# A decoder layer's delta rule on one core: triangular inverse merged to 128 rows, key norms from the Gram diagonal, local logits ahead of the inverse

## Chip, cores and metric

One Trainium2 chip, one of its cores. The metric is the device time of one execution in microseconds; it was 1342.42 us (median of three runs, 1338.79 to 1344.01).

## What is computed

One decoder layer in float32, 256 tokens of width 2048. The mixer has eight heads of a gated delta rule and eight heads of causal local attention; then come an output projection, cross-attention to 256 memory tokens, a gated MLP with a causal convolution, and norms. The change lies in the two kinds of mixer heads:

```
q, k, v = silu(conv(.)) per head;  k and q scaled to length 1
A = strictly lower part of (beta k) k^T * decay      (chunks of 64 tokens)
T = inverse of (I + A)
v_new = T (beta v) - T (beta k exp(G)) state
o = q exp(G) state + (q k^T * decay) v_new
state = state * exp(G_last) + (k exp(G_last - G))^T v_new
local head:  softmax(q k^T / sqrt(128) + bias) v, causal
```

The kernel uses two token blocks of 128 in place of four chunks of 64; the result is the same.

## The kernel before

All weights come once from HBM, 1 MB a transfer, into three raw buffers. A weight tile (a unit: 8 k-tiles of 128 columns, or 2 of 512) is split into a high part `hi` (ScalarE, ACT) and a rest `lo` (VectorE, DVE), each in a ring of four tiles. TensorE (PE) multiplies hi by the whole of the other side and lo by its high part: per k-tile one product of 512 columns and one of 256. These form the weight stream; `stream` (L275) writes it in order.

Everything else is written as jobs: Python generators (`k_evac`, `q_evac`, `v_evac`, `kb_evac`, `mem_job` and others) that yield wherever a result must come back from another engine. `Plan` (L48) keeps a rough clock of the engines while the program is written; `Jobs.tick` lets a job go on when its last result is due by that clock, so its instructions land between the products of the stream. All engines then run their instructions in the order in which they were written. The clock counts for a transfer 0.25 us and its size, and then 2.2 us until its data is there (`Plan.dma`).

The parts that matter here:

- Keys (`k_evac`, L572). After convolution and SiLU the squares of k (ACT) are summed over the channels by two products with a column of ones on PE; then come the Gram products k k^T of both token blocks, in the same bank.
- Inverse (`subst_job`, `u_job`, L616 and L653). DVE substitutes blocks of 32 rows; `u_job` joins two blocks of 32 to one of 64, with two pairs of products on PE. So `U` holds inverses of 64 rows.
- Values (`v_evac`, L727). For each of two token blocks a head applies the inverse: first 64 rows, a product with the off-diagonal block of 64, a subtraction, a product with the second inverse of 64, so three products with a copy or a subtraction after each; then the output and its norm (`out_norm`).
- Local attention (`kb_evac`, L821). A head waits until all inverses are there (`done["U"]`), makes logits, takes a tile of 128x512 from the pool `T5` (four tiles, tt0 to tt3) for bias, exponent and transposes, and multiplies by the values; heads 4 to 7 wait before that for all heads' `y`.
- Memory tokens (`mem_job`, `mem_piece`, L944 and L957). When heads of the delta rule are done, their tiles are reused for the transposed memory tokens, 16 k-tiles in tiles mT0 (0 to 5), mT1 (6 to 11) and mT2 (12 to 15). A piece is two k-tiles: it takes a T5 tile if another one is free too (`T5.get(1)`), SyncE (SP) transfers 256 KB into it, and ACT and DVE split it into mT. The four memory blocks of the stream (`mk_evac`), first k-tiles 0 to 7 of all four, then 8 to 15, follow the mixer's input projection. `when` holds the writing of a product back until its source has been written; on the chip PE then waits for it.

SP's queue holds both kinds of transfers: a weight load goes out when its raw buffer has been split, and the loads and pieces behind it wait for that.

Of the kernel before, what the change touches and what calls it, by code (L numbers as in the profile page):

```python
# [33 lines left out]
# columns of the small per-channel tensor  # L34
# [3 lines left out]
# columns of the constant tensor  # L38
# [9 lines left out]
class Plan:  # L48
    """A rough clock of the engines, kept while the program is written: a job goes on when its last
    result is due, so that no engine waits in its queue for another."""  # L50
# [17 lines left out]
    def dma(self, queue, size):  # L68
        """A transfer; returns when its data is there."""
        c, start = self.cur, max(self.t.get(queue, 0.0), self.now)  # L70
        if c is not None and c.eng != queue:
            start = max(start, c.end + SEM)
        self.t[queue] = start + 0.25 + size / 380e3
        if c is not None:
            c.end, c.eng = self.t[queue] + 2.2, queue
        return self.t[queue] + 2.2
# [107 lines left out]
def layer_kernel(ctx: ExitStack, tc: tile.TileContext, ins, out):  # L184
# [18 lines left out]
    # ---------------- tiles that live through the kernel  # L203
# [34 lines left out]
    # ---------------- the weight stream  # L238
# [56 lines left out]
    def w_unit(src, steps):  # L295
        """128-column blocks of weights as the stationary side, tokens moving; steps: (block, k)."""
        def tick(i):
            def f(u):
                for j in range(i, min(i + 2, len(steps))):
                    b, k = steps[j]  # L300
                    if k == 0:
                        b["ps"] = now(acc)
                    ps, last = b["ps"], k == b["k"] - 1
                    w = slice(j * P, (j + 1) * P)
                    xk = src(k)
                    if b["wide"]:
                        mm(ps, u.hi[:, w], xk, start=k == 0, stop=False)
                    else:
                        mm(ps[:, :256], u.hi[:, w], xk[:, :256], start=k == 0, stop=False)
                        mm(ps[:, :256], u.hi[:, w], xk[:, 256:], start=False, stop=False)  # L310
                    mm(ps[:, :256], u.lo[:, w], xk[:, :256], start=False, stop=last)
                    if last:
                        jobs.add(b["evac"](ps))
            return f
        return Unit(len(steps) * P, [tick(i) for i in range(0, len(steps), 2)])
# [20 lines left out]
    def s_block(src, kts, cols, evac, size=2, first=0):  # L336
        """Some k-tiles of weights per unit moving, the tokens stationary."""
        box = {}
        g = [kts[i:i + 1] for i in range(first)] + [kts[i:i + size] for i in range(first, len(kts), size)]
        return [Unit(len(ks) * cols, [s_part(src, ks, k, cols, box, ks is g[0], ks is g[-1]) for k in ks],  # L340
                     after=(lambda: evac(box["ps"])) if ks is g[-1] else None) for ks in g]

    def s_block_last(src, kts, cols, evac):
        """As s_block; the last units serve the first token block, and then the second."""
# [22 lines left out]
    # ---------------- small helpers  # L367
    def rstd_of(ss, n, w, tag=None):
        """(ss / n + eps) ** -0.5 for [P, w]."""
        r = stat(w, tag)  # L370
        vec.tensor_scalar(r, ss, 1.0 / n, EPS, op0=OP.mult, op1=OP.add)
        pool.tensor_tensor(r, r, pw[:, :w], op=OP.pow)
        return r

    def split(dst, ps, g=None):
        """PSUM [P, 256] -> high and low parts of dst [P, 512]."""
# [11 lines left out]
    # ---------------- start: constants, x, its norm and transposes  # L388
# [28 lines left out]
    # gst columns: 0:2 |k|^2 + eps, 2:4 beta / that, 6:8 its root, 10:12 |q|^2 + eps, 12:14 scale of q,  # L417
    # 14:16 sum of o^2, 16:20 the output's factor
    done = {"y": 0, "L": 0, "Q": 0, "U": 0, "T": False, "bt": False, "oT": 0, "oTm": 0, "d": 0, "mk": 0}

    # ---- w_in stream
    def when(key, ap):
        """The source of a product, once the program that writes it is there."""
# [123 lines left out]
    def conv_front(ps, blk, taps, dst_fn):  # L547
        """Evacuate a channel-major block, convolve over tokens, SiLU."""
# [23 lines left out]
    def k_evac(h):  # L572
        def f(ps):
# [11 lines left out]
            act.activation(t1[:, :256], kT, AF.Square)  # L585
            yield
# [3 lines left out]
            for tb in range(2):  # L590
                mm(ps[:, 384 + tb:385 + tb], t1[:, tb * P:(tb + 1) * P], ones[:, :1])
            mm(ps[:, :256], kT[:, :P], kT)
            mm(ps[:, 256:384], kT[:, P:], kT[:, P:])
            yield
            T.put(t1)
            vec.tensor_scalar(st[:, 0:2], ps[:, 384:386], EPS, None, op0=OP.add)
# [56 lines left out]
    def u_job(h):  # L653
# [16 lines left out]
        vec.tensor_tensor(u, u, ps[:, 256:].rearrange("p (b c) -> p b c", b=2), op=OP.subtract)  # L670
        aux.put(ps)
# [31 lines left out]
    def out_norm(ps, st, c_in, f_of, sink, g, z=None):  # L703
        """PSUM [tok, 2, 128] of one head -> RMS norm (and gate) -> channel-major high and low parts."""
        t = yield from T.get()
# [21 lines left out]
    def v_evac(h):  # L727
        def f(ps):
# [18 lines left out]
            for tb in range(2):  # L747
                c = slice(tb * P, (tb + 1) * P)
                lc = tb * 256
# [9 lines left out]
                act.activation(y[:64, c], ps[:64, :P], AF.Copy)  # L759
                yield  # L760
                mm(ps[64:, P:256], l[:64, lc + 64:lc + P], y[:64, c])
                yield
                vec.tensor_tensor(v[64:, c], v[64:, c], ps[64:, P:256], op=OP.subtract)
                yield
                mm(ps[64:, 256:384], u[64:, 64:], v[64:, c])
                yield
                act.activation(y[64:, c], ps[64:, 256:384], AF.Copy)
                yield
                aux.put(ps)
            T.put(v)  # L770
# [23 lines left out]
            yield from out_norm(ps, st, 14, f_of, sink, gcol(G_GDN, 0), [d[:, 384:], l[:, 384:512]])  # L794
# [26 lines left out]
    def kb_evac(h):  # L821
        def f(ps):
# [3 lines left out]
            while ("qb", h) not in box or not done["bt"] or done["U"] < H:  # L826
                yield
# [24 lines left out]
            while h >= H // 2 and done["y"] < H:  # L852
                yield
            ps = yield from aux.get()
# [23 lines left out]
            yield from out_norm(ps, st, 4, f_of, sink, gcol(G_MOBA, 0))  # L878
# [4 lines left out]
    # ---------------- residual blocks  # L883
    def resid_evac(n, ver, gbase, wide):
        """x += product, channel-major; high and low parts with the next norm's gain."""
# [13 lines left out]
    def x_rstd(ver):  # L899
        """The factors [P, 2] of the norm of x, from its channel-major blocks."""  # L900
# [24 lines left out]
    # ---------------- memory tokens  # L925
    def natural_ss(src, tile, ss):
        """Sums of squares of the rows [tokens, D], one 512-column piece in tile after another."""
# [121 lines left out]
    # ---------------- gated MLP  # L1049
# [61 lines left out]
    def final(tb, ps):  # L1111
        """The last columns of a token block, the final norm and the store."""
# [22 lines left out]
    # ================= the stream of weights, in the order of use  # L1135
# [76 lines left out]
    # ================= emission  # L1212
# [10 lines left out]
    def row_tile(r):  # L1223
        """The per-token factors r [P, 2] along the free axis, on every partition."""
# [120 lines left out]
# ---- host side: layouts only  # L1345
def _w(w):
    """[2048, 128 n] -> n blocks [2 halves, 128, 8 * 128]: the units of w_block."""
# [4 lines left out]
def _s(w):  # L1352
    """[k, 512 n] -> n blocks [k / 256, 128, 2 * 512]: the units of s_block."""
# [4 lines left out]
def _t(x):  # L1358
    """[tokens, D] -> [128, D / 128, tokens]."""
# [97 lines left out]
```

## Time and profile before

| | us |
|---|---|
| three runs | 1338.79, 1342.42, 1344.01 |
| profiled execution, span from first to last instruction | 1340.8 |
| PE busy in it | 1325.9 (99%) |
| DVE busy | 933.6 (70%) |
| ACT busy | 687.9 (51%) |
| GpSimd (POOL) busy | 53.0 (4%) |

The profiled execution has no time of its own beside its span. It is one execution, and busy time of PE is the union of its instructions, whose ends are modelled. In the timeline the distance from one start to the next is the better measure of what an instruction costs. All instructions are recorded under line 95, the line of the helper that issues them, so groups are told apart by tiles: bank is a PSUM bank, t and tt are scratch tiles, U and kt the inverses and their transposes, AB the heads' decay and Gram matrices, ytiles the values' y.

### The profile page before, as it was taken

Reading aid. Unit: us, or ns where it says so; the run is one execution under the profiler, and the core shown is the slowest. Engines: PE = TensorE matmul, PEld = TensorE weight load, DVE = VectorE, ACT = ScalarE, POOL = GpSimd, SP = SyncE. Lnnn points to the kernel's source line nnn. Section 1 sums busy time; section 2 is a strip of 40 time slices with the busy share of each in tenths; the row PEclk is TensorE's granted clock in tenths of the full one; section 3 lists DMA queues with packets and bytes.
Section 4 is the critical chain, followed back from the end, with each engine's and each line's share of the span. In section 5 each row is a group of like instructions: output and inputs, shape, how many; then the busy total and the mean of one; then the engine's idle time right before and its main releaser. Section 6 shows DMA issues by size and latency. Waiting matters only on the chain.

```text
span 1340.8 us, 19353 instructions
## 1 busy us (share of the span) xinstructions
PE 1325.9 (99%) x7414; PEld 1150.0 (86%) x7414; DVE 933.6 (70%) x1594; ACT 687.9 (51%) x1112; POOL 53.0 (4%) x140
## 2 busy tenths in 40 slices
PE   8999999999999999999999999999999999999997
PEld 7998888888888889998888888888888888888886
DVE  5688798968786766687777777545477777775554
ACT  5676554557564544465544444433344444444443
POOL 0101110201110000000000000000000000000000
PEclk9999999999999999999999999999999999999999
DMA  9666555534255654455455555555545555555552
GB/s 328 220 225 212 191 210 188 183 117 150 95 197 187 224 196 179 157 194 184 160 187 187 188 183 196 188 189 188 188 173 188 195 199 185 192 189 189 188 188 95
DMA packets 50793, 250.43 MB, mean 187 GB/s; under 512 B 11603, under 2 KB 15884, under 8 KB 23436
## 3 DMA queue, kind: packets, MB, share of 16 engines
q1 hardware_dynamic: 49152, 245.53, 51.5%
q0 software_dynamic: 448, 2.11, 0.4%
q10 hardware_dynamic: 1100, 1.54, 0.4%
q8 instruction: 58, 0.95, 0.3%
q14 instruction: 35, 0.29, 0.1%
HBM read 246.53 MB, written 2.64 MB: 186 GB/s over the span
## 4 chain that ended last, share of the span: by engine, by line
PE 54%; issue 0%; DVE 0%; ACT 0%; POOLq 0%; POOL 0%; ACTq 0%; DVEq 0%
PE bank L95 54%; ACT xn L95 0%; DVE lo L95 0%; ACT hi L95 0%; DVE xn L95 0%; DVE t L95 0%; POOLq L1453 0%; POOL stats L95 0%; DVE tt L95 0%; ACTq L95 0%; DVE stats L95 0%; DVEq L95 0%
## 5 line engine op out<-in xcount | busy, mean ns | idle before, releaser
L95 DVE TENSOR_TENSOR lo<-raw,hi 128x1024 fp32r<-128x1024 f32 (+4 forms) x449 | 540.2, 1205 | 349.1 <-ACT hi L95 344.8
L95 PE MATMUL bank<-xT,hi 128*128 128x512 f32 x2112 | 754.7, 400 | 0.3 <-DVE xT L95 0.3
L95 ACT ACTIVATE hi<-raw 128x1024 fp32r<-128x1024 f32 (+4 forms) x449 | 467.2, 1042 | 468.0 <-PE bank L95 357.7
L95 PE MATMUL bank<-xT,lo 128*128 128x256 f32 x2112 | 592.3, 280 | 0.0
L95 PEld LDWEIGHTS bank<-xT,hi 128*128 128x128 f32 x2112 | 396.3, 188 | 92.6 <-issue 2.6
L95 PEld LDWEIGHTS bank<-xT,lo 128*128 128x128 f32 x2112 | 399.3, 189 | 0.6
L95 PE MATMUL bank<-hi,actT 128*128 128x512 f32 x704 | 221.0, 395 | 0.0
L95 PEld LDWEIGHTS bank<-hi,actT 128*128 128x128 f32 x704 | 132.3, 188 | 31.5
L95 PE MATMUL bank<-lo,actT 128*128 128x512 f32 x352 | 139.0, 395 | 0.0
L95 PE MATMUL bank<-hi,xT 128*128 128x512 f32 (+3 forms) x320 | 87.2, 357 | 4.0 <-ACT xT L95 3.2
L95 DVE SCALAR_TENSOR_TENSOR t<-pad,sml,t 128x256 f32<-128x256 f32 x160 | 78.6, 491 | 8.5 <-DVE t L95 0.9
L95 PEld LDWEIGHTS bank<-lo,actT 128*128 128x128 f32 x352 | 66.2, 188 | 15.8
L95 ACT ACTIVATE t<-bank 128x256 f32<-128x256 f32 (+1 forms) x164 | 56.6, 348 | 21.4 <-PE bank L95 21.2
L95 PEld LDWEIGHTS bank<-hi,xT 128*128 128x128 f32 x320 | 57.4, 192 | 10.1 <-ACT xT L95 3.9
L95 ACT ACTIVATE t<-t,sml 128x256 f32<-128x256 f32 x44 | 22.3, 506 | 78.5 <-DVE t L95 78.4
L95 DVE TENSOR_TENSOR t<-bank,t 128x256 f32<-128x256 f32 x132 | 55.1, 417 | 3.4 <-ACT t L95 3.3
L95 PE MATMUL bank<-lo,xT 128*128 128x512 f32 (+3 forms) x160 | 56.3, 352 | 0.0
L95 POOL TENSOR_TENSOR stats<-stats,pw 128x2 f32<-128x2 f32 (+1 forms) x38 | 29.4, 775 | 557.5 <-DVE stats L95 557.5
L95 PE MATMUL bank<-oTm,hi 128*128 128x512 f32 x128 | 45.1, 394 | 0.0
L95 PE MATMUL bank<-oTg,hi 128*128 128x512 f32 x128 | 45.1, 393 | 0.0
L95 DVE TENSOR_TENSOR t<-t,t 128x256 f32<-128x256 f32 x96 | 41.0, 427 | 1.8
L95 PE MATMUL bank<-oTg,lo 128*128 128x256 f32 x128 | 36.2, 283 | 0.0
(157 smaller groups left out, 1053.8 us busy)
## 6 DMA issues: line engine op xcount, KB each, us to landing
raw<-wst SPq DMA_DIRECT2D x212, 1024.0 KB, 4.8
raw<-wz SPq DMA_DIRECT2D x4, 768.0 KB, 4.4
raw<-wz SPq DMA_DIRECT2D x3, 800.0 KB, 8.6
xn<-x SPq DMA_DIRECT2D x4, 512.0 KB, 8.4
raw<-wz SPq DMA_DIRECT2D x4, 512.0 KB, 4.4
tt<-mem SPq DMA_DIRECT2D x8, 256.0 KB, 5.1
tt<-memT SPq DMA_DIRECT2D x8, 256.0 KB, 5.9
xres<-xT SPq DMA_DIRECT2D x4, 512.0 KB, 5.8
```

The lines of the kernel that those rows point to most:

```text
L95: r = f(o, *a, **k)
```

## The change

1. `k_evac`: the squares on ACT and the two one-column products per head are gone. The norm is read off the Gram matrix: two DVE instructions multiply a 128x128 block of the bank by the identity and sum each row.
2. `u_job` goes on from 64 to 128 rows: two transposes of 64x64, a copy, two products of 64x64 with 64 columns, a copy, two more such products, a subtraction, for each head. `v_evac` then applies the inverse with one product per token block, and the two products of 64x64 with 128 columns, their copy and subtraction are gone.
3. `kb_evac` makes logits, exponent and transposes without the inverse, and waits for `done["U"]` after them; its tile for the norm is taken ahead of the bank. `out_norm` gets its tile from the caller, v in a head of the delta rule.

```diff
@@ k_evac
             t1, kT = yield from conv_front(ps, h, 4, lambda: box["kt"][:, h, :])
-            act.activation(t1[:, :256], kT, AF.Square)
-            yield
             while ("d", h) not in box:
                 yield
             ps = yield from aux.get()
-            for tb in range(2):
-                mm(ps[:, 384 + tb:385 + tb], t1[:, tb * P:(tb + 1) * P], ones[:, :1])
             mm(ps[:, :256], kT[:, :P], kT)
             mm(ps[:, 256:384], kT[:, P:], kT[:, P:])
             yield
+            for tb in range(2):
+                stt(t1[:, tb * P:(tb + 1) * P], ps[:, tb * 256:tb * 256 + P], 1.0, ident, OP.mult, OP.mult,
+                    accum_out=st[:, tb:tb + 1])
             T.put(t1)
-            vec.tensor_scalar(st[:, 0:2], ps[:, 384:386], EPS, None, op0=OP.add)
+            vec.tensor_scalar(st[:, 0:2], st[:, 0:2], EPS, None, op0=OP.add)
@@ u_job
         vec.tensor_tensor(u, u, ps[:, 256:].rearrange("p (b c) -> p b c", b=2), op=OP.subtract)
+        yield
+        for tb in range(2):
+            pe.transpose(ps[:64, tb * 64:tb * 64 + 64], U[:64, tb * H + h, :64], ident[:64, :64])
+        yield
+        act.activation(t[:64, :P], ps[:64, :P], AF.Copy)
+        yield
+        for tb in range(2):
+            mm(ps[64:, P + tb * 64:P + tb * 64 + 64], l[:64, tb * 256 + 64:tb * 256 + P], t[:64, tb * 64:tb * 64 + 64])
+        yield
+        act.activation(t[64:, :P], ps[64:, P:256], AF.Copy)
+        yield
+        for tb in range(2):
+            mm(ps[:64, 256 + tb * 64:256 + tb * 64 + 64], t[64:, tb * 64:tb * 64 + 64], U[64:, tb * H + h, 64:])
+        yield
+        w = U[:64, h:2 * H:H, 64:]
+        vec.tensor_tensor(w, w, ps[:64, 256:384].rearrange("p (b c) -> p b c", b=2), op=OP.subtract)
@@ v_evac
                 mm(ps[:, :P], u, v[:, c])
                 yield
-                act.activation(y[:64, c], ps[:64, :P], AF.Copy)
-                yield
-                mm(ps[64:, P:256], l[:64, lc + 64:lc + P], y[:64, c])
-                yield
-                vec.tensor_tensor(v[64:, c], v[64:, c], ps[64:, P:256], op=OP.subtract)
-                yield
-                mm(ps[64:, 256:384], u[64:, 64:], v[64:, c])
-                yield
-                act.activation(y[64:, c], ps[64:, 256:384], AF.Copy)
+                act.activation(y[:, c], ps[:, :P], AF.Copy)
                 yield
                 aux.put(ps)
-            T.put(v)
...
-            yield from out_norm(ps, st, 14, f_of, sink, gcol(G_GDN, 0), [d[:, 384:], l[:, 384:512]])
+            yield from out_norm(v, ps, st, 14, f_of, sink, gcol(G_GDN, 0), [d[:, 384:], l[:, 384:512]])
@@ kb_evac
-            while ("qb", h) not in box or not done["bt"] or done["U"] < H:
+            while ("qb", h) not in box or not done["bt"]:
                 yield
...
-            while h >= H // 2 and done["y"] < H:
-                yield
+            while done["U"] < H or (h >= H // 2 and done["y"] < H):
+                yield
+            t = yield from T.get()
             ps = yield from aux.get()
```

Since the jobs are written by the clock of `Plan`, the change moves many other instructions. Three places follow, as the programs have them; raw0 to raw2 are weight buffers, tt0 to tt3 the T5 tiles, memT the transposed memory tokens in HBM, mT0 to mT2 their split tiles; the number behind the underscore tells allocations of a name apart.

SP's queue at the end of the mixer's input projection, before:

```order
L95 DMA raw1_73<-wst 128x2048
L95 DMA tt2_104<-memT 128x512
L95 DMA tt3_105<-memT 128x512
L95 DMA raw2_74<-wst 128x2048
L95 DMA raw0_72<-wst 128x2048
L95 DMA tt1_103<-memT 128x512
L95 DMA tt2_104<-memT 128x512
L95 DMA tt3_105<-memT 128x512
L95 DMA raw1_73<-wst 128x2048
```

and now:

```order
L95 DMA raw0_72<-wst 128x2048
L95 DMA raw1_73<-wst 128x2048
L95 DMA tt0_102<-memT 128x512
L95 DMA tt1_103<-memT 128x512
L95 DMA raw2_74<-wst 128x2048
L95 DMA tt2_104<-memT 128x512
L95 DMA raw0_72<-wst 128x2048
L95 DMA tt1_103<-memT 128x512
L95 DMA raw1_73<-wst 128x2048
L95 DMA tt2_104<-memT 128x512
```

Both listings hold the last five of memT (mT1 and mT2). Before, two weight loads stood between the second and the third, and the last three followed each other; now a load stands ahead of each of the last three, and the last piece (tt2, k-tiles 14 and 15) stands behind a load of raw1.

PE in the first memory block, around k-tiles 6 and 7 (the first rows with mT1), before:

```order
L95 MATMUL bank5_111<-mT0_2846,lo1_80 128x256
L95 MATMUL bank5_111<-mT0_2846,hi1_76 128x512
L95 MATMUL bank5_111<-mT0_2846,lo1_80 128x256
L95 MATMUL bank0_106<-cst_68,tt0_102 128x128 x3
L95 MATMUL bank5_111<-mT1_3253,hi1_76 128x512
L95 MATMUL bank5_111<-mT1_3253,lo1_80 128x256
L95 MATMUL bank5_111<-mT1_3253,hi1_76 128x512
L95 MATMUL bank5_111<-mT1_3253,lo1_80 128x256
L95 MATMUL bank6_112<-cst_68,t10_94 128x128 x2
```

and now:

```order
L95 MATMUL bank5_111<-mT0_3071,hi1_76 128x512
L95 MATMUL bank5_111<-mT0_3071,lo1_80 128x256
L95 MATMUL bank5_111<-mT0_3071,hi1_76 128x512
L95 MATMUL bank5_111<-mT0_3071,lo1_80 128x256
L95 MATMUL bank5_111<-mT1_3327,hi1_76 128x512
L95 MATMUL bank5_111<-mT1_3327,lo1_80 128x256
L95 MATMUL bank6_112<-t6_90,t10_94 128x128
L95 MATMUL bank6_112<-t6_90,t10_94 128x256
L95 MATMUL bank5_111<-mT1_3327,hi1_76 128x512
L95 MATMUL bank5_111<-mT1_3327,lo1_80 128x256
```

Before, the two k-tiles follow each other; now a group of logits (t6, t10) stands between k-tile 6 and k-tile 7.

DVE around the splits of mT2 (k-tiles 12 to 15), before:

```order
L95 SCALAR_TENSOR_TENSOR mT2_3353<-tt2_104,sml_69,mT2_3353 128x256
L95 TENSOR_TENSOR lo3_82<-raw2_74,hi3_78 128x1024
L95 SCALAR_TENSOR_TENSOR mT2_3353<-tt3_105,sml_69,mT2_3353 128x256
L95 TENSOR_SCALAR t10_94<-bank6_112,stats_101 128x128 x2
L95 SCALAR_TENSOR_TENSOR mT1_3253<-tt1_103,sml_69,mT1_3253 128x256
L95 TENSOR_TENSOR lo0_79<-raw2_74,hi0_75 128x1024
L95 TENSOR_TENSOR t11_95<-bank1_107,t11_95 128x256
L95 SCALAR_TENSOR_TENSOR mT2_3353<-tt2_104,sml_69,mT2_3353 128x256
L95 SCALAR_TENSOR_TENSOR mT2_3353<-tt3_105,sml_69,mT2_3353 128x256
```

and now:

```order
L95 TENSOR_TENSOR lo3_82<-raw1_73,hi3_78 128x1024
L95 COPY tt0_102<-bank6_112 128x384
L95 TENSOR_TENSOR lo0_79<-raw1_73,hi0_75 128x1024
L95 RECIPROCAL stats_101<-stats_101 128x2
L95 TENSOR_TENSOR stats_101<-stats_101 128x2
L95 SCALAR_TENSOR_TENSOR stats_101<-stats_101 128x2
L95 TENSOR_SCALAR stats_101<-stats_101 128x2
L95 SCALAR_TENSOR_TENSOR mT2_3422<-tt1_103,sml_69,mT2_3422 128x256 x2
L95 TENSOR_SCALAR t8_92<-bank7_113,stats_101 128x128 x2
L95 SCALAR_TENSOR_TENSOR oTm1_3526<-bank7_113,sml_69,oTm1_3526 128x256
L95 SCALAR_TENSOR_TENSOR mT2_3422<-tt2_104,sml_69,mT2_3422 128x256 x2
```

Before, mT2 is written around the splits lo3 and lo0 of the units that PE starts on after 1792 and 1808 products of the stream; now it is written after lo3 and lo0 of the units at 1856 and 1872. PE wants k-tile 12 at product 1832 and k-tile 14 at 1836 in both.

## Rows read from the trace of the kernel before

**Rows 1.** The page, part 1: busy us (share of the span) xinstructions.

```profile
PE 1325.9 (99%) x7414; PEld 1150.0 (86%) x7414; DVE 933.6 (70%) x1594; ACT 687.9 (51%) x1112; POOL 53.0 (4%) x140
```

**Rows 2.** Windows, mid-program: stretch and length, PE, PEld, DVE, ACT, POOL, clock, DMA.

```profile
450.00:475.00 25.00, 25.00 (x144) 21.93 (x143) 16.77 (x23) 12.36 (x15) 0.00 (x0) 1.00 0.56 201
```

**Rows 3.** Waits of PE: waiter, releaser: total us, times, longest us.

```profile
PE bank L95 <- ACT xT L95: 3.2, 1, 3.2
```

**Rows 4.** Windows at the start, columns as in rows 2.

```profile
8.00:12.90 4.90, 0.99 (x5) 0.40 (x3) 2.38 (x4) 3.05 (x5) 0.00 (x0) 1.00 1.03 401
13.40:16.70 3.30, 3.30 (x12) 3.26 (x11) 3.26 (x6) 2.56 (x6) 0.00 (x0) 0.50 1.02 394
```

**Rows 5.** Timeline of PE: start us, us, instruction; Gram group and logits group.

```profile
109.55 0.50 PE L95 MATMUL bank<-ones,t 128*128 128x1 f32 x4
...
110.88 0.28 PE L95 MATMUL bank<-xT,lo 128*128 128x256 f32 x1
...
356.88 0.82 PE L95 MATMUL bank<-t,t 128*128 128x128 f32 x4
...
357.76 0.28 PE L95 MATMUL bank<-xT,lo 128*128 128x256 f32 x1
```

**Rows 6.** Timelines of DVE and PE: a split lo and its first use.

```profile
104.34 1.22 DVE L95 TENSOR_TENSOR lo<-raw,hi 128x1024 fp32r<-128x1024 f32 x1
...
106.72 0.40 PE L95 MATMUL bank<-xT,hi 128*128 128x512 f32 x1
```

**Rows 7.** Timeline of PE: runs of 64x64 in the stream.

```profile
320.30 0.28 PE L95 MATMUL bank<-xT,lo 128*128 128x256 f32 x1
320.51 0.43 PE L95 MATMUL bank<-ytiles,AB 64*64 64x128 f32 x2
...
321.21 0.28 PE L95 MATMUL bank<-xT,lo 128*128 128x256 f32 x1
...
287.23 1.08 PE L95 MATMUL bank<-ytiles,AB 64*64 64x128 f32 x8
...
288.58 0.28 PE L95 MATMUL bank<-xT,lo 128*128 128x256 f32 x1
```

**Rows 8.** Groups by form, whole program: xcount, busy us, mean ns, idle before.

```profile
L95 PE MATMUL bank<-t,U 64*64 64x128 f32 x32 | 5.8, 287 | 0.0
L95 PEld LDWEIGHTS bank<-ytiles,AB 64*64 64x64 f32 x32 | 3.2, 132 | 1.9 <-issue 0.7 <-ACT hi L95 0.3 <-ACT t L95 0.3
L95 PEld LDWEIGHTS bank<-ones,t 128*128 128x128 f32 x64 | 8.8, 190 | 0.9
L95 DVE SCALAR_TENSOR_TENSOR t<-bank,stats,AB 128x128 f32<-128x128 f32 x16 | 4.6, 344 | 0.8 <-POOL stats L95 0.8
L95 ACT ACTIVATE hi<-raw 128x1024 fp32r<-128x1024 f32 x424 | 448.6, 1059 | 455.3 <-PE bank L95 350.9 <-issue 88.8 <-ACT t L95 4.4
L95 ACT ACTIVATE mT<-tt,sml 128x256 fp32r<-128x256 f32 x16 | 7.5, 503 | 1.2 <-DMA tt<-memT 1.0
L95 DVE TENSOR_TENSOR lo<-raw,hi 128x1024 fp32r<-128x1024 f32 x424 | 519.5, 1226 | 334.1 <-ACT hi L95 329.8 <-PE bank L95 3.1
```

**Rows 9.** Timelines of DVE and PE: last split of mT, first use.

```profile
396.35 0.87 DVE L95 SCALAR_TENSOR_TENSOR mT<-tt,sml,mT 128x256 fp32r<-128x256 f32 x2
...
409.91 0.48 PE L95 MATMUL bank<-mT,hi 128*128 128x512 f32 x1
```

**Rows 10.** DMA issues: count, KB each, median us to landing.

```profile
raw<-wz SPq DMA_DIRECT2D x4, 768.0 KB, 4.4
raw<-wz SPq DMA_DIRECT2D x3, 800.0 KB, 8.6
tt<-memT SPq DMA_DIRECT2D x8, 256.0 KB, 5.9
```

**Rows 11.** Timelines of SP and ACT: three pieces of memT and the first's split.

```profile
382.92 1.58 SPq L95 DMA_DIRECT2D tt<-memT  x3
...
388.61 1.16 ACT L95 ACTIVATE mT<-tt,sml 128x256 fp32r<-128x256 f32 x2 [0.19 <-DMA tt<-memT]
```

More of the change, by code (lines that the diff above doesn't have):

```diff
@@ L701, in q_evac, with out_norm @@
         return f
-    def out_norm(ps, st, c_in, f_of, sink, g, z=None):
-        t = yield from T.get()
+    def out_norm(t, ps, st, c_in, f_of, sink, g, z=None):
         for tb in range(2):
@@ L748, in f @@
                 c = slice(tb * P, (tb + 1) * P)
-                lc = tb * 256
                 u = U[:, tb * H + h, :]
@@ L876, in sink @@
                 return box[n][:, h % 4, :]
-            yield from out_norm(ps, st, 4, f_of, sink, gcol(G_MOBA, 0))
+            yield from out_norm(t, ps, st, 4, f_of, sink, gcol(G_MOBA, 0))
             done["oTm"] += 1
```

## The prediction

> **What bounds the kernel now.** I read the page first. TensorE (PE) is busy for 1325.9 of 1340.8 us [rows 1], and the clock is full in its middle part [rows 2]. "Busy" can hide waits, since matmul ends are modelled, so I went to the waits of PE next: the longest single one is 3.2 us [rows 3], and it lies at the start, where PE has little to do [rows 4]. Then the timeline of PE, where I took times from start to start: in a plain stretch 144 products of the weight stream pass in 25 us [rows 2], 0.174 us each, and the small products of the attention are slipped in between with no gap that a wait would leave. So in the part that the change touches PE is the bound: an instruction taken from PE is worth its own length, and a wait put before one costs its whole length. What VectorE (DVE) and ScalarE (ACT) gain or lose is worth nothing while their splits of the weights stay ahead of PE.
>
> **The change, part by part.**
>
> *Norm of k.* Eight heads lose four one-column instructions each (two products, each issued as two). With them the inserted group lasts from 109.55 to 110.88 us, 1.33 us; a group that holds only the four logit instructions, of the same shapes as the four Gram instructions, lasts from 356.88 to 357.76, 0.88 us [rows 5]. That is 0.45 us a head, **3.6 us off PE**. ACT loses eight squares. DVE gets 16 products with the identity, priced like the nearest form that reads PSUM, 0.344 us [rows 8]: 5.5 us in all, 0.69 a head. I cost them at nothing. What hides them is DVE's lead: the thinnest that I found is the split that ends at 104.34 + 1.22 = 105.6 and is first used at 106.72 [rows 6], 1.2 us, and the new order puts two blocks of decay products, which stood ahead of that split, behind it. Without that lead the added 0.69 us a head would stall PE, 5.5 us in all.
>
> *The inverse.* Products of 64x64 are dear because of the change of shape. Two such instructions put 0.21 + 0.70 - 0.35 = 0.56 us into the stream, where 0.35 is what the two neighbours take without them (2 x 0.174); eight last from 287.23 to 288.58, 1.35 us against 0.70 for two, so one more costs 0.108 us and one run 0.56 - 2 x 0.108 = 0.34 us on top [rows 7]. Before there are 64 such instructions (two groups of 32, of which one stands in [rows 8]) in 20 runs, counted on the timeline: 64 x 0.108 + 20 x 0.34 = 13.7 us. The change removes all and adds 64 of 64 columns and 16 small transposes; in the new order they stand in 15 runs. The price of 64 columns is not in the trace. At most it is that of 128, 0.108; at least half, 0.054. I take the half, because the weight load of a 64x64 instruction is also shorter, 132 against 190 ns [rows 8], so it would not bind. So 80 x 0.054 + 15 x 0.34 = 9.4 us, **4.3 us off PE**; with the upper price 13.7, nothing gained. Three ACT and three DVE steps per half and head leave the chain of the values; PE never waited for them, so I give nothing for it.
>
> The Trainium skill, page "TensorEngine Tiling (Array Packing)", section "Restrictions and Gotchas", says that column tiling switches off the transpose mode for FP32. By it the 16 transposes would be issued as ordinary products, 16 instructions more, and the sum would be 16 x 0.054 = 0.9 us higher by my estimate. No row here shows a 64x64 transpose, and the sum goes without it.
>
> *Logits earlier.* They cost PE the same. But a head of local attention now takes its T5 tile, and keeps it, before it waits for the inverse. There are four such tiles, and the transposed memory tokens come in through them too, one piece only while another tile is free. In the new order three heads give theirs back within the last few stream products before the memory blocks, so the pieces come late: the splits of memT (tiles mT1 and mT2) now stand where PE is about to use them. Before, DVE's last such split ran at 396.35 while PE's first product with it starts at 409.91 [rows 9]; over 12 us of cover, and now it is gone. Two places:
>
> First place, k-tiles 6 and 7 of the first memory block. Count from the moment PE starts the product that frees tt1. PE: 12 instructions of 0.11, 4 stream products, 6 of 0.11, 4 stream products, 2 transposes, 10 stream products and a logits group (0.88 less one stream product of 0.24) make 1.3 + 0.7 + 0.7 + 0.7 + 0.2 + 1.7 + 0.65 = 6.0 us to the product that wants k-tile 7. The data: 0.7 for the read of tt1, 5.9 to land [rows 10], ACT's split for k-tile 8, which stands ahead, 0.50 [rows 8], then on DVE 0.44 for it (two take 0.87 in [rows 9]), 0.69 for two norm steps and 0.44 for k-tile 7 itself: 8.7 us. **PE waits 2.7 us.**
>
> Second place, k-tiles 14 and 15. Count from PE's start on the unit that uses them. PE: 3 x 0.11, 4 products, 6 x 0.11, 4 products, 4 products, 2 x 0.11: 3.3 us. The data: SyncE issues that transfer behind a weight load whose buffer is free once the unit before has been split, and that split takes a hi tile of the ring of four, free only when PE is at this very unit (ACT's hi waits above all for PE [rows 8]). So 1.06 for hi and 1.23 for lo [rows 8], 0.5 for the issue of the load ahead (three issues take 1.58 in [rows 11]), 5.9 to land, 0.50 and 0.44 for the split: 9.7 us. **PE waits 6.4 us**, the wait for k-tile 12 on the way included. Whoever is queued behind the waiting products on PE is the whole weight stream, so nothing makes this up later.
>
> Landing times in the trace go from 4.4 to 8.6 us for transfers of a few hundred KB [rows 10]; I take memT's own. With the ends the two waits are 1.2 + 4.9 = 6.1 us and 5.4 + 9.1 = 14.5 us.
>
> *Clock.* From 8.0 to 12.9 PE was busy for 0.99 of 4.9 us, and after it, from 13.4 to 16.7, the granted clock was 0.50, the 1.2 GHz level [rows 4]; half of those 3.3 us is lost, 1.7 us. At the second place PE would be busy for some 2 of 9 us, much alike, so I add **1.7 us**; ends 0 and, were both waits to bring it, 3.4.
>
> The Trainium skill, page "TensorE: Matmul & The Clock Gate", section "The HAM clock gate", says that the low level is the default and that activity releases the high one; the row agrees [rows 4]. By that rule, without the row, a fall is as likely.
>
> *Sum:* -3.6 - 4.3 + 2.7 + 6.4 + 1.7 = +2.9 us, against the profiled span of 1340.8: 1343.7. That span lies 1.6 us under the median of the three runs, 1342.42, so the forecast for the median is 1342.4 + 2.9 = **1345.3 us**. With the ends: -3.6 - 4.3 + 6.1 = -1.8 and -3.6 + 14.5 + 3.4 = +14.3.
>
> **The rivals.** A measurement of this kernel can tell about 0.5%, 6.7 us, from no change; the three runs alone differ by 5.2.
>
> 1. *The transfers are hidden after all.* If the memory tokens are in place before PE asks, only the saved instructions count: 1342.4 - 7.9 = 1334.5 us, faster. For it: before, PE shows no wait for mT, and every other inserted product was on time. Against it: the program order, in which the transfer is issued too late for its own landing time.
>
> 2. *Only the first wait is there*, for instance because the last weight load before the last transfer finds its buffer free early: -7.9 + 2.7 = -5.2, 1337.2 us, no difference that can be told.
>
> 3. *Slower: the landings are long.* Both places wait for a full landing, so each microsecond more counts twice. From a landing of 7.8 us (2 x 1.9 over memT's 5.9) the sum passes +6.7; with the 8.6 of the slowest row it is -7.9 + 14.5 + 1.7 = +8.3, 1350.7 us. For it: a 1 MB weight load is issued right ahead of the last transfer. Against it: such a load went ahead of the transfers at 382.92 as well, and ACT had the first one's data at 388.61 [rows 11].
>
> 4. *The change does not bring the logits forward.* The order excludes it: the first logits of local attention stand 92 stream products earlier.
>
> **How the numbers follow.** Forecast, both waits, between -1.8 and +6.7: 0.55. Rival 1: 0.15, its whole weight faster by over 0.5%. Rival 2: 0.10, within 0.5%. Rival 3, with dear 64-column products as its helper: 0.20, slower by over 0.5%. So faster 0.15, same 0.65, slower 0.20. The range that leaves out about 2 in 10 goes from 1336.5, just above rival 1 and with rival 2 inside, to 1351.5, past rival 3's 1350.7. For the forecast alone it is 1340.6 to 1349.1.
>
> **What would show it.** In the profile after: one-column k products gone, the Gram group at 0.88 us; the 64x64 instructions in 15 runs, at 0.054 each beyond the fixed 0.34; in the waits of PE, two new ones ended by DVE's mT, 2.7 us, and 6.4 us in two pieces, near 390 and 400 us; memT transfers issued by SyncE after that of before; a stretch at clock 0.50 behind the second. The prediction is wrong in its main step if PE has no wait for mT, and in its size if the waits exceed 14 us or the 64-column instructions cost 0.108.

## The result, and the profile after

17 runs of each: 1353.35 us (1344.54 to 1355.59) against 1343.25 (1337.08 to 1347.78), 10.1 us between the medians; the ratio is 1.0066 (95% interval 1.005 to 1.0081), which makes 8.9 us slower (6.7 to 10.9). The forecast was 1345.3, the range ended at 1351.5. The profiled execution took 1351.6 us from first to last instruction against 1340.8. The page of the profile, span and part 1, beside [rows 1]:

```profile
span 1351.6 us, 19355 instructions
...
PE 1326.9 (98%) x7398; PEld 1148.1 (85%) x7398; DVE 934.0 (69%) x1618; ACT 689.3 (51%) x1108; POOL 50.4 (4%) x140
```

PE's busy time rose by 1.0 us (what was saved is in it), the span by 10.8. The waits of PE, columns as in [rows 3]:

```profile
PE bank L95 <- DVE mT L95: 8.2, 4, 3.4
PE bank L95 <- ACT kt L95: 1.3, 1, 1.3
```

Both lines are new. The timeline of PE in the first memory block and around k-tiles 12 to 15 (start, us, instruction, idle time before it and what ended it):

```profile
390.18 0.28 PE L95 MATMUL bank<-mT,lo 128*128 128x256 f32 x1
393.33 0.50 PE L95 MATMUL bank<-mT,hi 128*128 128x512 f32 x1 [2.87 <-DVE mT L95]
...
395.16 0.80 PE L95 MATMUL bank<-mT,hi 128*128 128x512 f32 x1 [0.56 <-DVE mT L95]
...
410.07 0.50 PE L95 MATMUL bank<-mT,hi 128*128 128x512 f32 x1 [1.36 <-DVE mT L95]
...
411.53 0.44 PE L95 MATMUL bank<-cst,t 128*128 128x128 f32 x2 [0.45 <-DVE t L95]
415.41 0.80 PE L95 MATMUL bank<-mT,hi 128*128 128x512 f32 x1 [3.44 <-DVE mT L95]
```

At the first place PE stops at k-tile 6 for 2.87 us and at k-tile 7 for 0.56; at the second at k-tile 12 for 1.36, at two transposes for 0.45 and at k-tile 14 for 3.44: 8.7 us in five pieces; the 0.45 is a wait for t, the rest for mT. Behind either place PE works at the low clock. Windows of the profile after (columns as in [rows 2]), the last one far behind the change:

```profile
394.90:398.30 3.40, 3.14 (x11) 2.85 (x12) 1.94 (x5) 1.81 (x3) 0.00 (x0) 0.51 0.05 17
415.40:418.80 3.40, 3.39 (x11) 2.91 (x12) 1.18 (x2) 1.33 (x2) 0.00 (x0) 0.50 0.00 0
975.00:1231.00 256.00, 256.00 (x1437) 221.29 (x1436) 186.79 (x290) 123.52 (x179) 1.89 (x19) 1.00 0.52 187
```

PE works at half the clock for 3.4 us each time (3.14 of them busy the first time), so up to 1.7 us are lost each time. A stretch as long as the last one, at the same work, in the kernel before:

```profile
965.00:1221.00 256.00, 256.00 (x1461) 224.89 (x1460) 188.32 (x293) 124.93 (x181) 1.89 (x19) 1.00 0.54 191
```

Here PE takes 1437 instructions in 256 us, and took 1461 before, at a clock of 1.00 both times: 24 x 0.175 = 4.2 us. The program of that stretch differs only in the PSUM banks that it takes. So the 10.8 us come from two stretches. Up to PE's first product of the output projection (the first that reads tile oTg, 419.34 before, 426.18 now) the change costs 6.8 us, and 4.2 come between 975 and 1231 us.

Why the pieces were late, the two places differ. Timelines of DVE and ACT at the first:

```profile
388.89 1.23 DVE L95 TENSOR_TENSOR lo<-raw,hi 128x1024 fp32r<-128x1024 f32 x1 [0.52 <-ACT hi L95]
390.03 0.16 DVE L95 RECIPROCAL stats<-stats 128x2 f32<-128x2 f32 x1
...
392.77 0.51 DVE L95 SCALAR_TENSOR_TENSOR mT<-tt,sml,mT 128x256 fp32r<-128x256 f32 x1
```

```profile
389.61 1.32 ACT L95 ACTIVATE mT<-tt,sml 128x256 fp32r<-128x256 f32 x3
...
414.33 0.91 ACT L95 ACTIVATE mT<-tt,sml 128x256 fp32r<-128x256 f32 x2 [1.85 <-DMA tt<-memT]
```

ACT's half of k-tile 6 starts at 389.61, with no wait for its data. DVE comes to its own half at 392.77: between lie twelve small norm steps and two larger ones of other heads, which stand ahead of it in DVE's order and leave no gap. So at the first place PE waits for the order of DVE, not for a landing. At k-tile 14 (ACT, last row) it is the transfer. SP's timeline:

```profile
408.90 0.33 SPq L95 DMA_DIRECT2D raw<-wst  x1
409.28 0.42 SPq L95 DMA_DIRECT2D tt<-memT  x1
```

The piece goes out at 409.28, right behind the weight load that had to wait for its buffer, and ACT has it at 414.33, 5.1 us later.

The parts that save, in the timeline of PE (runs of 64x64 with 64 columns; the Gram group):

```profile
315.19 0.44 PE L95 MATMUL bank<-ytiles,AB 64*64 64x64 f32 x4
315.56 0.51 PE L95 MATMUL bank<-xT,hi 128*128 128x512 f32 x1
...
316.47 0.68 PE L95 MATMUL bank<-U,ytiles 64*64 64x64 f32 x8
317.07 0.51 PE L95 MATMUL bank<-xT,hi 128*128 128x512 f32 x1
```

```profile
96.96 0.81 PE L95 MATMUL bank<-kt 128*128 128x256 f32 x4
97.53 0.48 PE L95 MATMUL bank<-xT,hi 128*128 128x512 f32 x1
97.84 0.28 PE L95 MATMUL bank<-xT,lo 128*128 128x256 f32 x1
```

Eight 64-column instructions last 316.47 to 317.07, four last 315.19 to 315.56: 0.23 us for four more, 0.058 each. They stand in 15 runs. The Gram group, counted to the xT,lo product behind it as in [rows 5], goes from 96.96 to 97.84: 0.88 us, as the group of the same shapes there. Against the stream's neighbours on both sides it costs 0.66 where the old one cost 1.10, so 0.44 a head.

### The profile page after: what moved, and what is told of

Read it like the earlier page. It is cut to its first block, busy times and chain, and to the rows that moved or that the text cites. A ratio compares the mean times of both kernels' runs of the same rounds, so it can differ in the third digit from the quotient of the medians.

```text
span 1351.6 us, 19355 instructions
## 1 busy us (share of the span) xinstructions
PE 1326.9 (98%) x7398; PEld 1148.1 (85%) x7398; DVE 934.0 (69%) x1618; ACT 689.3 (51%) x1108; POOL 50.4 (4%) x140
## 4 chain that ended last, share of the span: by engine, by line
PE 54%; issue 0%; DVE 0%; ACT 0%; POOLq 0%; POOL 0%; ACTq 0%; DVEq 0%
PE bank L95 54%; ACT xn L95 0%; DVE lo L95 0%; ACT hi L95 0%; DVE xn L95 0%; DVE t L95 0%; POOLq L1458 0%; POOL stats L95 0%; DVE tt L95 0%; ACTq L95 0%; DVE stats L95 0%; DVEq L95 0%
```

## Experiments

Beside medians, the table gives places in the trace that are finer than a median: when DVE starts the substitution and the sixth delta-rule output (oTg; with it heads 3 to 5 are done, whose tiles mT1 reuses), when SP issues the fourth piece of memT (the first of mT1), what PE waits for mT, and when PE starts the output projection. All in us. The first 48 us, in which nothing was changed, differ from one execution to another: the column "start" says how much later than before the 201st product of the stream starts (47.60 before). That much is also in the column of the projection. Each ratio is against runs of the kernel before on the same chip; the medians come from several chips.

| | start | subst. | sixth oTg, DVE | 4th piece | waits for mT | projection, PE | median (runs) | ratio, 95% |
|---|---|---|---|---|---|---|---|---|
| before | 0 | 160.1 | 362.0 | 368.7 | 0 | 419.3 | 1343.25 (17) | |
| whole change | -0.5 | 166.1 | 368.8 | 382.3 | 8.2 | 426.2 | 1353.35 (17) | 1.005 to 1.0081 |
| e1 Gram alone | -0.7 | 166.1 | 394.2 | 404.2 | 4.8 | 441.9 | 1367.6 (6) | 1.0153 to 1.0216 |
| e2 logits alone | 0.7 | 161.2 | 370.8 | 377.7 | 0 | 421.4 | 1343.95 (12) | 0.9986 to 1.0024 |
| e3 inverse, logits | 0.7 | 161.1 | 362.3 | 366.8 | 0 | 417.0 | 1343.12 (12) | 0.9964 to 1.0012 |
| e4 whole, pieces first | -0.7 | 166.3 | 368.9 | 374.1 | 0 | 412.9 | 1340.38 (12) | 0.9963 to 1.0 |
| e5 Gram, short subst. | -0.8 | 165.8 | 361.5 | 366.2 | 0 | 416.8 | 1339.92 (10) | 0.9974 to 0.9992 |
| e6 Gram, pieces first | -1.0 | 167.1 | 389.6 | 388.1 | 6.9 | 430.3 | 1358.05 (4) | 1.0104 to 1.0144 |
| e7 whole, short subst. | 0.8 | 167.3 | 352.7 | 360.5 | 0 | 415.3 | 1338.52 (7) | 0.9961 to 0.9989 |
| e8 both mends | -1.4 | 165.7 | 350.8 | 358.6 | 0 | 415.1 | 1340.16 (12) | 0.9978 to 1.0001 |
| e9 before, late subst. | -0.9 | 178.0 | 383.2 | 398.0 | 7.6 | 442.8 | 1369.72 (4) | 1.0167 to 1.021 |
| e12 no early logits | 0.0 | 166.7 | 349.1 | 349.1 | 0 | 413.2 | 1336.32 (12) | 0.9948 to 0.9975 |

**The parts alone (e1, e2, e3).** e1 is the kernel before with the first diff, e2 with the second, and e3 is the whole change with the first diff undone:

```diff
@@ k_evac
-            act.activation(t1[:, :256], kT, AF.Square)
-            yield
...
-                mm(ps[:, 384 + tb:385 + tb], t1[:, tb * P:(tb + 1) * P], ones[:, :1])
...
+                stt(t1[:, tb * P:(tb + 1) * P], ps[:, tb * 256:tb * 256 + P], 1.0, ident, OP.mult, OP.mult,
+                    accum_out=st[:, tb:tb + 1])
```

```diff
@@ kb_evac
-            while ("qb", h) not in box or not done["bt"] or done["U"] < H:
+            while ("qb", h) not in box or not done["bt"]:
...
-            while h >= H // 2 and done["y"] < H:
+            while done["U"] < H or (h >= H // 2 and done["y"] < H):
```

> The kernel before with the Gram diagonal alone; inverse and logits as before. Measure: when PE starts on the first product of the output projection (tile oTg), 419.3 us before and 426.2 with the whole change. Tiles theory (the early logits hold the T5 tiles, so the memory pieces come late; the prediction's): no wait of PE for mT, oTg near 419.3 - 3.6 = 415.7, and with the wait for kt that came with the change (1.3 us) 417; 1339.5 us in all against 1343.25. Start theory (without the squares of k the order lets the last decay product of the keys come later, so the substitution starts some 6 us later than before, and the heads of the delta rule, whose tiles the memory tokens need, end later): PE waits for mT as in the whole change, 8 us and more with the clock, though the logits are not moved; oTg at 422 to 428.

> The kernel before with the early logits alone. Tiles theory: PE waits for mT, 5 to 10 us, oTg at 424 to 429, 1348 to 1353 us. Start theory: the substitution starts as before, the order has each piece of memT split at least 30 stream products (5 us) ahead of its use, so PE does not wait for mT; oTg at 419 to 420.5, 1343 us.

> The whole change without the Gram diagonal (squares of k on ACT and one-column products as before). Tiles theory: the waits for mT stay, 8 us, oTg at 426 to 430. Start theory: no wait for mT, and what is left is the saving of the merged inverse, which the prediction put at 4.3 us: oTg near 415, 1339 us. If the inverse saves nothing, oTg stays at 419.3.

The tiles theory missed all three, the start theory met the second. The third had no wait either, but came at 417.0 where 415 was expected. The Gram diagonal without early logits is 24.7 us slower, far worse than the whole change; waits of PE in e1:

```profile
PE bank L95 <- DVE t L95: 5.4, 8, 1.5
PE bank L95 <- DVE mT L95: 4.8, 4, 1.9
```

More than these waits is lost in e1: PE is busy for 17.5 us at a clock of 0.50 between 397.7 and 435.2, which is 8.8 us. The early logits alone bring no wait. e3 against e2 (both with early logits and the same start): 417.0 - 421.4 = -4.4 us, the merged inverse's own worth (with the tile for `out_norm`, which changed with it). e2 against before: 2.0 us, 0.7 of them in the start, so 1.3 us for the early logits; 0.5 of that arise near 180 us, where the second trace of before (e10) shows 0.4 too, so 0.9 to 1.3 us. With the Gram diagonal the substitution starts 6 us later. DVE before, then with the whole change, the first substitution step and the fifth and sixth oTg:

```profile
160.08 1.38 DVE L95 TENSOR_TENSOR sub<-sub 128x496 f32<-128x496 f32 x2 [3.13 <-DMA sub<-lscr]
...
361.61 0.87 DVE L95 SCALAR_TENSOR_TENSOR oTg<-bank,sml,oTg 128x256 fp32r<-128x256 f32 x2
```

```profile
166.09 1.39 DVE L95 TENSOR_TENSOR sub<-sub 128x496 f32<-128x496 f32 x2 [0.57 <-DMA sub<-lscr]
...
368.43 0.87 DVE L95 SCALAR_TENSOR_TENSOR oTg<-bank,sml,oTg 128x256 fp32r<-128x256 f32 x2
```

The last key's decay products do not make the 6 us: DVE starts on them at 143.41 before and at 145.03 now. Their four transfers to lscr make most of it. SP before, then with the whole change, with the weight load ahead:

```profile
142.93 0.33 SPq L95 DMA_DIRECT2D raw<-wst  x1
...
145.71 2.87 SPq L95 DMA_DIRECT2D lscr<-AB  x4
```

```profile
153.47 0.33 SPq L95 DMA_DIRECT2D raw<-wst  x1
153.85 1.83 SPq L95 DMA_DIRECT2D lscr<-AB  x4
```

They go out 8.1 us later. Counted on SP's rows they stand behind the 34th weight load now, before behind the 32nd, and the 34th had to wait for DVE to split its buffer, until 153.45. So a step that comes 1.6 us later has got a place two loads further back in SP's queue.

**Only the start moved (e9).** Nothing of the change is in it:

```diff
-                jobs.add(subst_job(), sp.due - plan.now, True)
+                jobs.add(subst_job(), sp.due - plan.now + 18.0, True)
```

> The kernel before with nothing of the change: only the substitution is put off, by one number (18 us of the planner's clock after the last key's transfers, which moves its start there from 160.6 to 178.3 and the end of the inverses from 277.6 to 289.2; with the Gram diagonal alone they end at 288.3). Start theory: the memory pieces come as late as with the Gram diagonal alone, PE waits for mT, oTg at 430 to 445, 1355 to 1370 us. Rival (something else in the Gram diagonal makes the heads late): no or small waits, oTg at 419 to 424.

```profile
PE bank L95 <- DVE mT L95: 7.6, 3, 5.4
PE bank L95 <- DVE t L95: 5.1, 6, 2.7
```

The rival fell: 442.8, as in e1, with the same two waits. A late inverse is enough by itself, whatever made it late. It is not only memT: 5.1 us are waits of PE for t, the heads' scratch tiles, and PE is busy for 14.5 us at a clock of 0.50, 7.2 us lost.

**The inverse made early again (e5, e7).** e5 is e1, e7 is the whole change, both with the substitution in fewer pieces. The late start stays, the end comes earlier (last step at 225 to 227 us, 252 in the whole change):

```diff
-            if r < 10 or r % 3 == 0:
+            if r % 4 == 0:
                 yield
```

> The Gram diagonal alone as in the first experiment, which came 24 us late at the output projection's end, but the substitution is written in fewer pieces (it yields after every fourth row from the first on, where it yielded after each of the first ten and then after every third): it starts as late as there, but is over earlier. Start theory: the heads end about as early as in the kernel before, the order has each piece of memT split 78 stream products or more ahead of its use, no wait for mT, and what is left is the saving of the diagonal less the wait for kt: oTg at 419.3 - 3.6 + 1.3 = 417, plus what DVE's longer stretches without a split cost PE near 170 us (0 to 6 us). Rival: it is something in the Gram diagonal itself (its steps on DVE) that makes the heads late; then the waits stay and oTg is above 430.

> The whole change with the substitution in fewer pieces (a yield after every fourth row), nothing else: the logits hold the T5 tiles as before. Start theory: pieces split 94 products or more ahead of their use, no wait for mT, oTg at 413 to 414 as with the pieces ahead of the logits, or up to 6 us later where DVE's longer stretches hold up a split near 170 us; 1338 to 1342 us. Tiles theory: the logits still take the tiles first, 3 us of wait or more stay, oTg above 417.

All waits for mT are gone in both, and e5's 416.8 is where it was expected. e7 shows that the logits may take the tiles as they like if heads and pieces are early: heads 3 to 5 are done at 352.7, 16 us earlier than in the whole change. e7's 415.3 is 1.3 us above the 413 to 414 hoped for, 0.8 of them from the start.

**The tiles given to the pieces (e4, e6).** The whole change, and e1, with the spare counts exchanged:

```diff
-            lg = yield from T5.get()
+            lg = yield from T5.get(1)
...
-        t = yield from T5.get(1)
+        t = yield from T5.get()
```

> The whole change, but a memory piece takes a T5 tile as soon as one is free, and the logits take one only while another is free (the two spare counts are exchanged). Tiles theory: the waits for mT go or fall below 2 us, oTg at 426.2 - 8 to - 10, 416 to 418, some 1340 us. Start theory: the heads end as late as in the whole change, so most of the waits stays, 5 us or more, oTg at 423 to 426.

> The Gram diagonal alone, with the spare counts of the T5 tiles exchanged as in the run that put pieces ahead of logits. If it is the T5 tiles that hold the pieces back whenever the heads are late, the waits go here too, oTg at 417 to 420. If the heads themselves are too late here (the order has the pieces no earlier than 8 to 14 products ahead of their use), oTg stays at 430 or more.

In e4 the tiles theory was right and the start theory wrong: all waits are gone. The heads end as late as in the whole change. DVE's fifth and sixth oTg in e4, then SP's row of the fourth and fifth piece in e4 and in the whole change:

```profile
368.52 0.87 DVE L95 SCALAR_TENSOR_TENSOR oTg<-bank,sml,oTg 128x256 fp32r<-128x256 f32 x2
```

```profile
374.13 4.37 SPq L95 DMA_DIRECT2D tt<-memT  x2
```

```profile
382.31 4.16 SPq L95 DMA_DIRECT2D tt<-memT  x2
```

The same piece goes out 8.2 us earlier, with the heads done at the same time: in the whole change 13.5 us pass from the sixth oTg to the fourth piece, in e4 5.2. In both it leaves SP 0.4 us behind a weight load, the 66th in the whole change and the 65th in e4 (the 63rd in before and in e3): the exchange put it one load ahead. In e6 the exchange gains 11.5 us over e1 and is not enough: heads 3 to 5 are done only at 389.6, and PE still waits 6.9 us for mT.

So neither theory holds alone. A late inverse makes the heads late, and with them the pieces (e1, e9). In the whole change the pieces lose a further place to the logits, which hold T5 tiles that they need (e4). Heads as late as that are not enough (e2: sixth oTg at 370.8, fourth piece 6.9 us later, no wait), nor are early logits. Either mend removes the waits of the whole change.

Whether it is the *early* logits that hold the tiles, e4 doesn't say. DVE's starts on the logits of the fifth to seventh local head in the whole change, and PE's last products that read them:

```profile
374.18 0.73 DVE L95 SCALAR_TENSOR_TENSOR tt<-bank,stats,ED 128x128 f32<-128x128 f32 x2
...
376.34 0.74 DVE L95 SCALAR_TENSOR_TENSOR tt<-bank,stats,ED 128x128 f32<-128x128 f32 x2
...
379.28 0.73 DVE L95 SCALAR_TENSOR_TENSOR tt<-bank,stats,ED 128x128 f32<-128x128 f32 x2
```

```profile
385.73 1.06 PE L95 MATMUL bank<-ED,tt 128*128 128x128 f32 x8
...
387.33 0.83 PE L95 MATMUL bank<-ED,tt 128*128 128x128 f32 x6
```

Three tiles are taken here at once; before, the same logits followed each other at 365.0, 376.7 and 390.7. But the last step of the inverse had started at 320.2 and ACT had copied the last y at 361.3, so the wait that the third part moved was over when these heads took their tiles. And e6 gains by the exchange without early logits. A run that undoes the third part alone and leaves the substitution as it is was not made, so what the early logits add to the waits is not shown. e1, without the second and third part, is 15.7 us later at the projection than the whole change: the two together shorten the loss.

**Both mends, and no early logits (e8, e12).** e12 is e7 with the third part undone:

```diff
-            while ("qb", h) not in box or not done["bt"]:
+            while ("qb", h) not in box or not done["bt"] or done["U"] < H:
```

> The whole change with both mends, the substitution in fewer pieces and the pieces ahead of the logits. Both theories: no wait for mT; oTg no earlier than with either mend alone (413), since a piece that is in place is in place; 1338 to 1341 us.

> The change without its third part (the logits wait for the inverses again), with the substitution in fewer pieces as in the whole change with that mend. The order has each piece of memT split 94 products or more ahead of its use. Start theory: no wait for mT. If the early logits cost PE something of their own (the logits alone had oTg 2 us late), oTg comes 1 to 2 us earlier than with them, 413.5 to 414.5 against 415.3, and the time is 1337 to 1338.5; if they are free, 415.3 and 1338.5.

In e8 no wait for mT came back, as expected, but with the start taken off its projection is 2.0 us later than e7's and 2.9 us later than e4's: both mends together cost something. e12 has the lowest median: 1336.32 us, 0.9962 of before (0.9948 to 0.9975), 5.1 us. Its projection starts here, and that of e7 here:

```profile
413.20 0.39 PE L95 MATMUL bank<-oTg,hi 128*128 128x512 f32 x1
```

```profile
415.27 0.39 PE L95 MATMUL bank<-oTg,hi 128*128 128x512 f32 x1
```

2.1 us apart, 0.7 of them from the start. Of the other 1.4, most is one wait of PE, which e7 has and e12 hasn't:

```profile
343.48 0.49 PE L95 MATMUL bank<-ytiles,AB 128*128 128x128 f32 x2 [1.16 <-ACT ytiles L95]
```

e2 and the whole change have no such wait, so this is another cost than e2's 1.3 us, of nearly the same size.

**Second traces (e10, e11).** The two kernels again, unedited:

> The kernel before, once more, for a second trace. Two explanations of the 4.2 us that the whole change lost between 975 and 1231 us, where its program is that of before: by the execution (each stretch of pairs of products goes at 346.7 or at 353.4 ns a pair, whichever kernel it is): then this trace may show 353.4 there, and oTg stays at 419 +- 1. By the change: 346.7 here.

> The whole change, once more, for a second trace. The waits for mT stand in the program's order, so they come again, 8 us with the half clock behind them, oTg at 425 to 428. The pairs of products between 975 and 1231 us go at 346.7 or 353.4 ns, by the execution; if by the change, at 353.4 again.

The projection starts at 419.6 and 426.5, so the 6.8 us repeat. The pairs of products between 975 and 1231 us go at 346.7 ns in both traces of before and at 353.4 in both of the change (from start to start over 675 pairs: 234.0 and 238.5 us), so the rate goes with the kernel and not with the execution. Of the other traces, e2, e5, e6, e7, e9 and e12 have 346.7 and e1, e3, e4 and e8 353.4. e7 has all that e4 has of the change, and e3 lacks the Gram diagonal: no part of the change sets it by itself. The PSUM banks are the one known difference between the programs there, and no run changed them alone; what sets the rate stays open.

## Why the prediction was wrong

*What held.* PE was the bound, and the waits came at the two places named, ended by DVE's mT. Their length was 3.4 and 5.3 us, 8.7, where 2.7 and 6.4, 9.1, stood. The merged inverse is worth 4.4 us by e3 (4.3 predicted), with 0.058 us for an instruction of 64 columns (0.054), and stands in 15 runs in the whole change; in e3 it stands in 17, for which the prediction's prices give 3.6, so 0.8 us have no term. The Gram group saves 0.44 us a head (0.45). The landing of the last piece was 5.1 us (5.9), so rival 3's long landings did not come; its time was passed in another way. That 8.7 lies so near 9.1 is partly luck: at the first place the prediction had PE wait 2.7 us at k-tile 7 for a landing, and PE waited 2.87 at k-tile 6 for DVE's norm steps, and only 0.56 at k-tile 7. Two slips in the working change nothing: the terms of the second place's data add up to 9.6, not 9.7, and the first product of [rows 6] takes hi, so DVE's lead there is 0.2 us longer.

*The step that failed: "Logits earlier".* It put the late pieces on the early logits, which take a T5 tile before they wait for the inverse, and keep it. Logits do hold tiles that the pieces need (e4), but early logits by themselves bring no wait (e2), and those that held the tiles had no inverse left to wait for. The step that was costed at nothing, "Norm of k", starts it (e3, e5, e7, e9): the last key's transfers come to stand two weight loads further back in SP's queue, the substitution starts 6.0 us later, and the fourth piece goes out at 382.3 in place of 368.7. I priced the Gram diagonal by its instructions and by DVE's lead, and did not follow its place in the order to the substitution.

The step "The inverse" gave nothing for the shorter chain of the values, and asked nothing for the longer one of the inverse. DVE starts on the last step of the inverse at 283.7 before and at 320.2 now (312.3 in e3, whose start is as before), and ACT copies the last y at 359.5 and 361.3: 36.5 us longer in front, 34.7 shorter behind.

What took the time past the range is not the waits for the pieces, which were 0.4 us less than forecast, but four sizes: 1.3 for kt and 1.3 for the early logits (by e2), both put at nothing, 1.7 more for the clock, and 4.2 beyond the projection.

*Terms missed or mis-sized*, up to the projection (+2.9 predicted, +6.8 measured):

- A wait for kt, 1.3 us by the waits (1.4 by the starts). Before, ACT had done the last of the decay's exponents by 110.9; now the last one comes behind a load of ACT's function table, and two keys' SiLU wait for another load (1.28 us each). ACT's timeline before and after, and PE's after:

```profile
110.45 0.40 ACT L95 ACTIVATE AB<-AB 128x256 f32<-128x256 f32 x1
```

```profile
115.48 1.28 ACT L95 ACT_TABLE_LOAD   x1
116.77 0.40 ACT L95 ACTIVATE AB<-AB,stats 128x128 f32<-128x128 f32 x1
...
134.79 1.28 ACT L95 ACT_TABLE_LOAD   x1
136.09 0.72 ACT L95 ACTIVATE kt<-t 128x256 f32<-128x256 f32 x2
```

```profile
136.56 0.92 PE L95 MATMUL bank<-kt 128*128 128x256 f32 x4 [1.25 <-ACT kt L95]
```

I had counted what the Gram diagonal takes off ACT, and not what it reorders there; e1 has the same wait. The load at 134.79 costs ACT 1.30 us from start to start.

- The early logits "cost PE the same": 0.9 to 1.3 us (e2). How much of it the whole change has is not shown.
- PE worked at the low clock behind both places, 3.4 us lost; 1.7 was taken, 3.4 was the bound.

With the waits' 8.7 these give -3.5 - 4.4 + 1.3 + 1.3 + 8.7 + 3.4 = 6.8 us. With the start taken off, the change costs 7.3 us up to the projection, and 7.8 between the second traces, where PE is busy for 9.7 us at a clock of 0.50 in place of 6.6: 0.5 to 1.0 us stay without a term.

*Beyond the projection*, 4.2 us of the profiled difference stand in a stretch that the change does not touch; no step had a term for it. Rival 1, the hidden transfers, gave 1334.5: the whole change with a mend (e4, e7, e8) takes 1338.5 to 1340.4 (of the three only e7's interval leaves out "no change"), and up to 2.6 us of the distance are the kt wait and the early logits' own cost.

The Trainium skill, page "TensorEngine Tiling (Array Packing)", section "Restrictions and Gotchas", says that column tiling and the transpose mode for FP32 exclude each other; read as in the prediction, the 64x64 transposes would be issued as ordinary products. The trace differs from that reading: 16 transposes are 16 instructions, where an FP32 product takes two. Groups by form, after:

```profile
L95 PE MATMUL bank<-cst,U 64*64 64x64 f32 x16 | 2.0, 226 | 0.0
```

## What to carry to other kernels

Where a planner writes the program, price an edit by what it does to the order's long chains (here keys, substitution, inverse, heads, tiles, transfers) before its instructions: the same part saves 3.5 us of PE and, alone, makes the kernel 24.7 us slower. Look above all at transfers that share a queue with loads: a step that ends 1.6 us later sent its data 8.1 us later. A transfer that needs a buffer from one chain and a tile that another holds has two ways to be late, so test them apart, undo each part of the change by itself, and try the change with its order mended before judging it. Compare traces at one product of the stream; that shows 2 us where medians of a dozen runs don't.

## What was not expected of the hardware

The same pairs of products, 512 and 256 columns, ran at 346.7 or at 353.4 ns a pair through 250 us at a granted clock of 1.00, and kept to it through the whole stretch. In 675 pairs that is 4.5 us, as much as the merged inverse is worth. Which one a kernel gets did not follow from its parts here. Between 640 and 860 us, where the stream has such pairs too, all fourteen traces have 353.3.

Two pauses of PE, of some 5 and 7 us with little work in them, were both followed by 3.4 us of work at a clock of 0.50, the 1.2 GHz level, as the one at the start had been [rows 4].
